# Root-mean-square norms over channels: a full-matrix mean on all partitions and a root by logarithm and exponential, in place of per-token columns and a broadcast

## The chip, the cores and the metric

The kernel runs on one core of a Trainium2 chip. The metric is device time in microseconds (us). Three runs of the kernel before took 2551.5, 2551.55 and 2554.44 us, so the median is 2551.55 us. One further run, of 2548.32 us, was profiled; its span, from the first to the last recorded instruction, is 2546.5 us. The engines are named as in the profile: PE (TensorE; PEld are its weight loads), DVE (VectorE), ACT (ScalarE), POOL (GpSimd), and SP, which only issues DMA transfers.

## The reference

One decoder layer over 2048 tokens of 1024 channels, all in float32. Four norms act on a token's 1024 channels: before the mixers, before the MLP, and at the end (three gains `g1`, `g2`, `g3`; the head norms over 64 channels are another routine that the change leaves alone).

```python
def rmsnorm(x, gain):
    y = x * lax.rsqrt(jnp.mean(x * x, axis=-1, keepdims=True) + EPS)
    return y * gain

h = rmsnorm(x, norm_mix_gain)             # 1
z = h @ w_in                              # 3072 columns, three mixers run on its parts
x = x + y @ w_out
x = x + conv_ffn(rmsnorm(x, norm_ffn_gain), w_up, conv_w, w_down)   # 2
x = x + sigmoid(x @ w_gate) * (p @ w_proj)
return rmsnorm(x, final_norm_gain)        # 3
```

## The kernel before

Channels lie on the 128 partitions (a token's 1024 channels are eight tiles, `KD = 8`) and tokens along the free axis. The 2048 tokens are two halves of `TH = 1024`, worked one after the other, and each half is two chunks of `CH = 512`. Every large product is three float32r matmuls (`mm3`, lines 261 to 264): both operands are split into a high and a low part, and the low times low product is left out. A split (`split`, line 253) is a rounding copy on ACT (line 255) and a subtraction on DVE or POOL (line 256). Weights are loaded on SP into the raw buffers `wr` (three) and `q` (three) and split two to three products ahead of their use (`w_get`, line 240).

A half has these stages:

- Input norm and projection. In half 0 the tokens are loaded at the start (`x_load`); `h_apply` (line 413) writes `hx = x * gain * rstd` on DVE (line 417) and splits it, some of the low parts on POOL. For half 1 the sums of squares are made from reloaded tokens while half 0 is in its MLP (`stats_steps`, line 980), and the norm is applied while half 0 is in its last stage. The projection is woven with the three mixers.
- Output projection (`out_evac`, line 760): x is reloaded by POOL's queue into `xr`, added to the product (line 765), squared for the second norm and stored by the same queue. While chunk 1 runs, the norm of chunk 0 is applied (`h2_first`); the norm of chunk 1 comes at the head of the MLP (`up_first`, line 881), where `h2_second` (line 786) forms normed tiles, their differences and their splits on DVE, ACT and POOL, and PE multiplies them as they come.
- MLP (`up`, `down_pair`, `down_last`), where PE has a long run of products.
- Gate, per-layer embedding and final norm (line 1036 on): two chunks of 512 tokens in half 0; 512, 256 and 256 in half 1. The last 256 tokens' norm ends the program.

There are 13 norms over channels, 11 of 512 tokens and 2 of 256: two at the start, two before the MLP in each half, two from `stats_steps`, two and three at the end of the halves. Each is an object of class `Norm`. `add` squares a tile on ACT and adds it to the accumulator on DVE or POOL. `rstd` multiplies each 128 tokens of the accumulator, as weights, by a column of ones (line 313), so that a token's sum lands on its own partition in a 128x4 tile; scale, root, reciprocal and a Newton step run there on DVE (lines 316 to 322) and ACT (line 317). `bcast` multiplies the root, repeated along the free axis as weights, by the identity (line 329), which puts it on all partitions in PSUM, where `pr` is read by line 417, 775 or 1028.

The order of instructions on each engine is set by a scheduler when the program is built; an engine takes its instructions strictly in that order. Small tiles (`hx`, `xr`, `xs`, squares) share the pool `sp` under the tag `t2`, four buffers.

Of the kernel before, what the change touches and what calls it, by code (L numbers as in the profile page):

```python
# [9 lines left out]
F32 = mybir.dt.float32  # L10
F32R = mybir.dt.float32r
I32 = mybir.dt.int32
AF = mybir.ActivationFunctionType
# [3 lines left out]
P = 128  # L17
# [3 lines left out]
CH = 512  # L21
NC = TH // CH
D = 1024
# [5 lines left out]
EPS = 1e-6  # L29
# [7 lines left out]
VOFF = {}  # L37
# [11 lines left out]
def trunk(ctx, tc, xT, pT, w_in, w_out, w_up, w_down, w_pp, w_pg, wr_bd, wi_bd, vecs, consts, masks, out):  # L49
    nc = tc.nc  # L50

    cp = ctx.enter_context(tc.tile_pool(name="cp", bufs=1))
    wp = ctx.enter_context(tc.tile_pool(name="wp", bufs=3))
    bp = ctx.enter_context(tc.tile_pool(name="bp", bufs=40))
    dp = ctx.enter_context(tc.tile_pool(name="dp", bufs=1, space=bass.MemoryType.DRAM))
    sp = ctx.enter_context(tc.tile_pool(name="sp", bufs=4))
    mm = ctx.enter_context(tc.tile_pool(name="mm", bufs=2, space=bass.MemoryType.PSUM))
    sm = ctx.enter_context(tc.tile_pool(name="sm", bufs=4, space=bass.MemoryType.PSUM))

    ACT = nc.scalar.activation  # L60
    TT = nc.vector.tensor_tensor
    TS = nc.vector.tensor_scalar
    STT = nc.vector.scalar_tensor_tensor
    MUL, ADD, SUB = ALU.mult, ALU.add, ALU.subtract
    MM = nc.tensor.matmul
# [3 lines left out]
    def nm(s):  # L69
        uid[0] += 1  # L70
        return f"{s}_{uid[0]}"

    def t4(name="t4", dt=F32):
        return bp.tile([P, TH], dt, tag="b", name=nm(name))
# [6 lines left out]
    def t2(name="t2"):  # L81
        return sp.tile([P, CH], F32, tag="t2", name=nm(name))
# [4 lines left out]
    def ps1(n=CH, name="ps1"):  # L87
        return sm.tile([P, n], F32, tag="sm", name=nm(name))
# [5 lines left out]
    pools = {}  # L94
# [39 lines left out]
        return kc(w_up[i * NJ + j])[:, QS[k]]  # L134

    def raw_q(src):
        raw = pools["ff"].tile([P, CH], F32, tag="q", name=nm("q"), bufs=3)
        dst = raw if len(src.shape) == 2 else raw.rearrange("p (a b) -> p a b", b=src.shape[2])
        nc.sync.dma_start(dst, src)
        return raw  # L140
# [50 lines left out]
    def last_job(hf, j):  # L191
        def load():
            raws[hf, j, 3] = raw_q(quarter(j, 1, 1))

        return (4, hf, j), load, lambda: one(raws[hf, j, 3])

    def down_jobs(hf, gi):
        js = GROUPS[gi]
        per = 4 // len(js)
        jobs = []  # L200
        for i in range(KD // per):
            def load(i=i):
                src = w_down[i * per : (i + 1) * per, :, js[0] : js[-1] + 1, :].rearrange("m p j c -> p m (j c)")
                raws[hf, gi, "d", i] = raw_q(src)
            jobs.append((("d", hf, gi, i), load, lambda i=i: one(raws[hf, gi, "d", i])))
        return jobs
# [22 lines left out]
    def w_upto(n):  # L229
        while wpos[1] < min(n, len(wlist)):  # L230
            key, _, make = wlist[wpos[1]]
            while wpos[0] <= wpos[1]:
                load = wlist[wpos[0]][1]
                wpos[0] += 1
                if load:
                    load()
            wpos[1] += 1
            wmade[key] = make()
# [14 lines left out]
    def split(hi, lo, src, eng=None):  # L253

        i = ACT(hi, src, AF.Copy)  # L255
        last_split[:] = i, (eng or nc.vector).tensor_tensor(lo, src, hi.bitcast(F32), op=SUB)  # L256
# [25 lines left out]
    ident = kt[:, KIDENT : KIDENT + P]  # L282
    onecol = kt[:, KONES : KONES + 1]
    blk = cp.tile([P, P], F32R, name="blk")
    vt = cp.tile([P, NV], F32, name="vt")

    def vec(name, i):
# [1 line left out]
        return vt[:, o : o + 1]  # L289

    epsc = cp.tile([P, 1], F32, name="epsc")


    class Norm:
# [4 lines left out]

        def add(self, src, eng=None, big=False):  # L300
            n = src.shape[-1]
            sq = (t4("sq") if big else t2("sq"))[:, :n]
            ACT(sq, src, AF.Square)
            if self.acc is not None:
                (eng or nc.vector).tensor_tensor(self.acc, self.acc, sq, op=ADD)
            else:
                self.acc = sq

        def rstd(self):
            n = self.acc.shape[-1] // P  # L310
            pm = ps1(n, "pm")
            for t in range(n):
                MM(pm[:, t : t + 1], self.acc[:, t * P : (t + 1) * P], onecol, start=True, stop=True)
            v = sp.tile([P, 16], F32, tag="tiny", name=nm("v"), bufs=4)
            m, r, s, u = (v[:, 4 * i : 4 * i + n] for i in range(4))
            TS(m, pm, 1.0 / D, EPS, op0=MUL, op1=ADD)
            ACT(s, m, AF.Sqrt)
            nc.vector.reciprocal(r, s)
            TT(u, r, r, op=MUL)
            TT(u, u, m, op=MUL)  # L320
            TS(u, u, -0.5, 1.5, op0=MUL, op1=ADD)
            TT(r, r, u, op=MUL)
            self.r = r

        def bcast(self):
            n = self.r.shape[-1]
            pr = ps1(n * P, name="pr")
            for t in range(n):
                MM(pr[:, t * P : (t + 1) * P], self.r[:, t : t + 1].to_broadcast([P, P]), ident, start=True, stop=True)
            return pr  # L330

    def head_norm(y, gain, scale=1.0):

# [95 lines left out]


    nc.vector.memset(epsc, EPS)
    warm = cp.tile([P, 1], F32, name="warm")
    ACT(warm, epsc, AF.Sqrt)
    h = [[None] * KD for _ in range(NC)]
    x0 = [[], []]

    def x_load(xs, hf, c, eng):

        t0 = hf * TH + c * CH
        for k in range(0, KD, 2):  # L440
            t = t4("xl")
            eng.dma_start(t.rearrange("p (k t) -> p k t", k=2), xT[k : k + 2, :, t0 : t0 + CH].rearrange("k p t -> p k t"))
            xs += [t[:, :CH], t[:, CH:]]
# [2 lines left out]
    nc.sync.dma_start(kt, consts[:, :KBLK])  # L446
    w_upto(1)
    nc.sync.dma_start(vt, vecs)
    w_upto(2)
    x_load(x0[1], 0, 1, nc.sync)  # L450
    norms = [Norm(), Norm()]
# [3 lines left out]
    pr = norms[0].bcast()  # L455
# [6 lines left out]
    for hf in range(NH):  # L462
# [5 lines left out]
        for i in range(NC):  # L468
            t = mx.tile([P, 8, P], F32, name=nm("acc"))
            nc.gpsimd.memset(t, 0.0)  # L470
            accs.append(t)
        for i in range(2):
            t = mx.tile([P, 8, 2, C], F32, name=nm("qz"))
# [256 lines left out]
        if first:  # L730
# [6 lines left out]
            t = t4("blk")[:, :P]  # L737
# [278 lines left out]
        for i in range(2):  # L1016
            raw = wp.tile([P, D], F32, tag="wr", name=nm("wr"))
# [18 lines left out]
        for ci, (t0, n) in enumerate(chunks):  # L1036
            c, o = t0 // CH, t0 % CH
            sl = slice(t0, t0 + n)
            raw, phi, plo = t4("pr"), t4("ph", F32R), t4("pl", F32R)
# [9 lines left out]
            for m in range(KD):  # L1049
# [6 lines left out]
                for k in range(KD):  # L1056
                    t = xs[c][k]
# [102 lines left out]
```

## Time and profile before

| | |
|---|---|
| median of three runs | 2551.55 us |
| profiled execution, its span | 2548.32 us, 2546.5 us |
| PE busy | 2454.9 us (96% of the span) |
| DVE busy | 1613.4 us (63%) |
| ACT busy | 1310.7 us (51%) |
| POOL busy | 237.2 us (9%) |
| mean granted TensorE clock | 0.987 of full speed |

Busy time is the time in which at least one instruction of the engine runs. Matmuls overlap in the trace: each of 512 columns lasts about 0.39 us, and the next begins 0.23 us after it. "Idle before" in square brackets is how long the engine had nothing to run ahead of a row, and the arrow names what ended it. A row with x4 stands for four instructions in a row.

### The profile page before, as it was taken

The numbers are of one execution on the slowest core, as the hardware profiler recorded it, in microseconds if no ns is written. First come the engines' busy times: TensorE is split into PE (matmuls) and PEld (weight loads), VectorE is DVE, ScalarE is ACT, GpSimd is POOL, SyncE is SP. The second block draws the span as 40 slices with busy tenths as digits, with TensorE's granted clock in tenths as the row PEclk, the third lists the DMA queues.
The fourth block names the chain that finished last, engine by engine and source line by source line (L and its number), as shares of the span: only waits on it lengthen the run. The fifth ranks groups of instructions, "written<-read, shape, count | busy, mean of one in ns | idle before, by whom it ended". The sixth has DMA issues, their size and how long they took to land. (4 is left out here: it accounts for less than half of the span.)

```text
span 2546.5 us, 30816 instructions
## 1 busy us (share of the span) xinstructions
PE 2454.9 (96%) x12004; PEld 2020.1 (79%) x12004; DVE 1613.4 (63%) x2384; ACT 1310.7 (51%) x1778; POOL 237.2 (9%) x278
## 2 busy tenths in 40 slices
PE   6999999899999999999999999997999999999998
PEld 4887788678888888887888887785888888888788
DVE  6666565685556566558666656567666666655776
ACT  5444884365555545555344457634555555555453
POOL 2000001201111111110110000012111111111100
PEclk9999999899999999999999999998999999999999
DMA  3101114346565555573421111251555555556642
GB/s 136 42 26 34 42 58 164 122 120 138 132 137 135 140 124 124 127 195 116 149 92 34 34 34 54 79 189 39 124 129 136 133 125 128 133 130 136 177 149 92
DMA packets 121170, 280.71 MB, mean 110 GB/s; under 512 B 11840, under 2 KB 42176, under 8 KB 121024
## 3 DMA queue, kind: packets, MB, share of 16 engines
q0 software_dynamic: 31360, 113.26, 21.3%
q1 hardware_dynamic: 88656, 164.30, 19.9%
q8 instruction: 94, 1.54, 0.2%
q10 hardware_dynamic: 1008, 1.18, 0.2%
q14 instruction: 52, 0.43, 0.1%
HBM read 178.03 MB, written 100.66 MB: 109 GB/s over the span
## 5 line engine op out<-in xcount | busy, mean ns | idle before, releaser
L262 PE MATMUL pz<-h,wh 128*128 128x512 f32 x768 | 306.3, 399 | 9.5 <-ACT h L255 9.5
L263 PE MATMUL pz<-h,wh 128*128 128x512 f32 x768 | 302.0, 394 | 1.2 <-DVE h L256 0.8
L264 PE MATMUL pz<-h,wl 128*128 128x512 f32 x768 | 300.6, 392 | 0.0
L262 PE MATMUL pdn<-ahi,wt 128*128 128x512 f32 x704 | 277.7, 394 | 12.6 <-DVE x L974 11.0
L264 PE MATMUL pa<-h,wt 128*128 128x512 f32 x704 | 276.5, 393 | 6.8 <-DVE wt L256 6.8
L262 PE MATMUL pa<-h,wt 128*128 128x512 f32 x704 | 276.3, 393 | 3.3 <-ACT wt L255 1.8
L263 PE MATMUL pdn<-alo,wt 128*128 128x512 f32 x704 | 275.8, 392 | 0.0
L264 PE MATMUL pdn<-ahi,wt 128*128 128x512 f32 x704 | 275.6, 392 | 0.0
L263 PE MATMUL pa<-h,wt 128*128 128x512 f32 x704 | 275.6, 391 | 0.0
L961 ACT ACTIVATE st<-pdn 128x1024 f32<-128x1024 f32 x160 | 164.0, 1026 | 210.5 <-PE pdn L264 189.9
L256 DVE TENSOR_TENSOR wt<-s,wt 128x512 fp32r<-128x512 f32 x168 | 114.1, 688 | 218.0 <-ACT wt L255 217.8
L962 POOL DMA_DIRECT2D xd<-st x160 | 136.9, 856 | 1087.4 <-ACT st L961 1084.3
L262 PEld LDWEIGHTS pz<-h,wh 128*128 128x128 f32 x768 | 144.8, 189 | 40.7 <-ACT h L255 10.7
L263 PEld LDWEIGHTS pz<-h,wh 128*128 128x128 f32 x768 | 144.8, 189 | 33.0 <-DVE h L256 4.1
L262 PEld LDWEIGHTS pdn<-ahi,wt 128*128 128x128 f32 x704 | 133.2, 189 | 45.6 <-DVE x L974 13.9
L264 PEld LDWEIGHTS pz<-h,wl 128*128 128x128 f32 x768 | 144.8, 189 | 30.1 <-issue 0.3
L256 DVE TENSOR_TENSOR wl<-wr,wh 128x1024 fp32r<-128x1024 f32 x120 | 146.2, 1227 | 35.1 <-ACT wh L255 34.7
L264 PEld LDWEIGHTS pa<-h,wt 128*128 128x128 f32 x704 | 133.3, 189 | 35.3 <-DVE wt L256 7.7
L262 PEld LDWEIGHTS pa<-h,wt 128*128 128x128 f32 x704 | 133.1, 189 | 33.0 <-ACT wt L255 2.7
L264 PEld LDWEIGHTS pdn<-ahi,wt 128*128 128x128 f32 x704 | 133.2, 189 | 28.0
L263 PEld LDWEIGHTS pa<-h,wt 128*128 128x128 f32 x704 | 133.1, 189 | 27.6
L263 PEld LDWEIGHTS pdn<-alo,wt 128*128 128x128 f32 x704 | 133.3, 189 | 27.1
(271 smaller groups left out, 5170.0 us busy)
## 6 DMA issues: line engine op xcount, KB each, us to landing
xd<-st POOLq DMA_DIRECT2D x160, 512.0 KB, 6.1
wr<-in_w_up SPq DMA_DIRECT2D x176, 256.0 KB, 4.1
wr<-in_w_in SPq DMA_DIRECT2D x48, 512.0 KB, 3.7
q<-in_w_down SPq DMA_DIRECT2D x88, 256.0 KB, 3.4
wr<-in_w_pg SPq DMA_DIRECT2D x40, 512.0 KB, 4.5
wr<-in_w_out SPq DMA_DIRECT2D x32, 512.0 KB, 3.8
q<-in_w_up SPq DMA_DIRECT2D x42, 256.0 KB, 3.0
xr<-in_xT POOLq DMA_DIRECT2D x32, 256.0 KB, 3.9
```

Source lines behind the costliest of these rows:

```text
L256: last_split[:] = i, (eng or nc.vector).tensor_tensor(lo, src, hi.bitcast(F32), op=SUB)
L262: MM(ps, wk[0], rk[0], start=start, stop=False, **kw)
L263: MM(ps, wk[0], rk[1], start=False, stop=False, **kw)
L264: MM(ps, wk[1], rk[0], start=False, stop=stop, **kw)
L961: ACT(st, ps, AF.Copy)
L962: nc.gpsimd.dma_start(xd[m], st, accum_op=ADD)
```

## The change

`Norm.add` gives the accumulator buffers of its own (tag `acc`, four of 512 columns); the first square goes there. `rstd` splits the accumulator into two float32r parts and multiplies both by a 128x128 matrix of 1/1024 (`ones`), so that the mean stands on all partitions for all tokens at once, in one PSUM tile. From it ACT forms the logarithm, the exponential of minus a half of it times a constant, and its square; two DVE instructions over the whole tile are a Newton step for the root. The sign comes out negative, so the three gains are negated once at the start. `bcast` returns the accumulator, in SBUF, and has no instructions. The pool `sp` goes from four buffers to three and `q` from three to two.

```diff
-    sp = ctx.enter_context(tc.tile_pool(name="sp", bufs=4))
+    sp = ctx.enter_context(tc.tile_pool(name="sp", bufs=3))
...
-        raw = pools["ff"].tile([P, CH], F32, tag="q", name=nm("q"), bufs=3)
+        raw = pools["ff"].tile([P, CH], F32, tag="q", name=nm("q"), bufs=2)
...
         def add(self, src, eng=None, big=False):
             n = src.shape[-1]
-            sq = (t4("sq") if big else t2("sq"))[:, :n]
+            if self.acc is None:
+                sq = sp.tile([P, CH], F32, tag="acc", name=nm("acc"), bufs=4)[:, :n]
+            else:
+                sq = (t4("sq") if big else t2("sq"))[:, :n]
             ACT(sq, src, AF.Square)
...
         def rstd(self):
-            n = self.acc.shape[-1] // P
+            n = self.acc.shape[-1]
+            t = t4("sqs", F32R)
+            split(t[:, :n], t[:, CH : CH + n], self.acc)
             pm = ps1(n, "pm")
-            for t in range(n):
-                MM(pm[:, t : t + 1], self.acc[:, t * P : (t + 1) * P], onecol, start=True, stop=True)
-            v = sp.tile([P, 16], F32, tag="tiny", name=nm("v"), bufs=4)
-            m, r, s, u = (v[:, 4 * i : 4 * i + n] for i in range(4))
-            TS(m, pm, 1.0 / D, EPS, op0=MUL, op1=ADD)
-            ACT(s, m, AF.Sqrt)
-            nc.vector.reciprocal(r, s)
-            TT(u, r, r, op=MUL)
-            TT(u, u, m, op=MUL)
-            TS(u, u, -0.5, 1.5, op0=MUL, op1=ADD)
-            TT(r, r, u, op=MUL)
-            self.r = r
+            MM(pm, ones, t[:, :n], start=True, stop=False)
+            MM(pm, ones, t[:, CH : CH + n], start=False, stop=True)
+            ACT(self.acc, pm, AF.Ln, bias=epsc)
+            ACT(self.acc, self.acc, AF.Exp, scale=-0.5, bias=lnc)
+            u = t4("nr")[:, :n]
+            ACT(u, self.acc, AF.Square)
+            STT(u, pm, EPS, u, op0=ADD, op1=MUL)
+            STT(self.acc, u, 1.5 * 2.0 ** (1 / 3), self.acc, op0=SUB, op1=MUL)
 
         def bcast(self):
-            n = self.r.shape[-1]
-            pr = ps1(n * P, name="pr")
-            for t in range(n):
-                MM(pr[:, t * P : (t + 1) * P], self.r[:, t : t + 1].to_broadcast([P, P]), ident, start=True, stop=True)
-            return pr
+            return self.acc
...
+    nc.vector.memset(lnc, -np.log(2.0) / 3)
     warm = cp.tile([P, 1], F32, name="warm")
-    ACT(warm, epsc, AF.Sqrt)
+    ACT(warm, epsc, AF.Square)
+    t = t2("ones")[:, :P]
+    nc.vector.memset(t, 1.0 / D)
+    ACT(ones, t, AF.Copy)
...
     nc.sync.dma_start(vt, vecs)
+    TS(vt[:, VOFF["g1"] : VOFF["gm"]], vt[:, VOFF["g1"] : VOFF["gm"]], -1.0, None, op0=MUL)
```

Lines of the changed kernel behind the class `Norm` have numbers seven to nine higher. The order of the instructions, at three places. First ACT at the start of the program, before the change: `wh` are split weights, `xl` the loaded tokens (`xl_111` to `xl_117` are chunk 1), `v` the 128x4 tile, `h` the split normed tokens of chunk 0.

```order
L255 ACTIVATE wh_100<-wr_98 128x1024
L317 ACTIVATE v_147<-v_147 128x4
L255 ACTIVATE wh_107<-wr_105 128x1024
L303 ACTIVATE sq_160<-xl_111 128x512
L303 ACTIVATE sq_180<-xl_117 128x512
L255 ACTIVATE h_185<-hx_183 128x512
```

The same place after it (`xl_118` to `xl_124` are chunk 1, `acc_126` is chunk 0's accumulator, `acc_161` that of chunk 1; as above, the squares between the first and the last are left out):

```order
L255 ACTIVATE wh_114<-wr_112 128x1024
L308 ACTIVATE acc_161<-xl_118 128x512
L255 ACTIVATE sqs_149<-acc_126 128x512
L322 ACT_TABLE_LOAD
L322 ACTIVATE acc_126<-pm_152,epsc 128x512
L325 ACT_TABLE_LOAD
L325 ACTIVATE acc_126<-acc_126,lnc 128x512
L327 ACTIVATE nr_157<-acc_126 128x512
L308 ACTIVATE sq_163<-xl_118 128x512
L308 ACTIVATE sq_181<-xl_124 128x512
L255 ACTIVATE h_186<-hx_184 128x512
```

The norm of chunk 0 now has a square of chunk 1 ahead of it on ACT, and seven squares of chunk 1 stand between it and the first split of `hx`. Second, DVE at the same place, before and after: `wl` are the low parts of the weights.

```order
L305 TENSOR_TENSOR sq_119<-sq_119,sq_139 128x512
L316 TENSOR_SCALAR v_147<-pm_142 128x4
L256 TENSOR_TENSOR wl_101<-wr_98,wh_100 128x1024
L318 RECIPROCAL v_147<-v_147 128x4
L322 TENSOR_TENSOR v_147<-v_147 128x4
L256 TENSOR_TENSOR wl_108<-wr_105,wh_107 128x1024
L417 SCALAR_TENSOR_TENSOR hx_183<-xl_89,vt,pr_155 128x512
```

```order
L310 TENSOR_TENSOR acc_126<-acc_126,sq_146 128x512
L455 TENSOR_SCALAR vt<-vt 128x24
L256 TENSOR_TENSOR wl_107<-wr_104,wh_106 128x1024
L256 TENSOR_TENSOR wl_115<-wr_112,wh_114 128x1024
L256 TENSOR_TENSOR sqs_149<-acc_126,sqs_149 128x512
L328 SCALAR_TENSOR_TENSOR nr_157<-pm_152,nr_157 128x512
L329 SCALAR_TENSOR_TENSOR acc_126<-nr_157,acc_126 128x512
L419 SCALAR_TENSOR_TENSOR hx_184<-xl_95,vt,acc_126 128x512
```

The first weights' low part no longer stands behind an instruction of the norm. Third, ACT at the head of the MLP of half 1, where the second norm before the MLP is made (`zg`, `zu` are evacuated products, `pa` their PSUM tiles, `x_12430` and `x_12389` the last tile of x); before, then after:

```order
L303 ACTIVATE sq_12781<-x_12430 128x512
L317 ACTIVATE v_12817<-v_12817 128x4
L890 ACTIVATE zu_12798<-pa_12795 128x512
L895 ACTIVATE zg_12797<-pa_12794 128x512
L255 ACTIVATE h_12849<-h_1925_12540 128x512
```

```order
L308 ACTIVATE sq_12734<-x_12389 128x512
L902 ACTIVATE zg_12750<-pa_12747 128x512
L255 ACTIVATE sqs_12765<-acc_12428 128x512
L322 ACT_TABLE_LOAD
L322 ACTIVATE acc_12428<-pm_12768,epsc 128x512
L325 ACT_TABLE_LOAD
L325 ACTIVATE acc_12428<-acc_12428,lnc 128x512
L327 ACTIVATE nr_12773<-acc_12428 128x512
L897 ACTIVATE zu_12751<-pa_12748 128x512
```

An evacuation (line 902) now stands ahead of the norm on ACT, the norm has four passes over 512 columns and two table loads, and the other evacuation stands behind it.

## Rows read from the trace of the kernel before

**Rows 1.** Busy time by stretch: PE, PEld, DVE, ACT, POOL, clock, DMA share, GB/s

```profile
560.00:1000.00 440.00, 439.02 (x1938) 362.52 (x1937) 254.76 (x352) 229.63 (x312) 53.90 (x63) 1.00 0.59 134
1720.00:1760.00 40.00, 29.04 (x118) 21.53 (x119) 30.04 (x42) 14.31 (x25) 15.06 (x11) 0.88 0.09 33
```

**Rows 2.** Timeline of PE around a broadcast: start, us, engine, line, operation

```profile
1687.54 1.05 PE L329 MATMUL pr<-kt,v 128*128 128x128 f32 x8
1688.35 0.48 PE L262 MATMUL po<-ys,wh 128*128 128x512 f32 x1
1688.66 0.40 PE L263 MATMUL po<-ys,wh 128*128 128x512 f32 x1
1688.89 0.39 PE L264 MATMUL po<-ys,wl 128*128 128x512 f32 x1
```

**Rows 3.** Timeline of the start: SP, ACT, DVE and PE

```profile
12.21 1.87 PE L313 MATMUL pm<-kt,sq 128*128 128x1 f32 x8 [12.21 <-DVE sq L305]
14.19 1.23 DVE L256 TENSOR_TENSOR wl<-wr,wh 128x1024 fp32r<-128x1024 f32 x1
15.82 2.06 SPq L442 DMA_DIRECT2D xl<-in_xT  x4
20.93 1.15 ACT L303 ACTIVATE sq<-xl 128x512 f32<-128x512 f32 x2 [5.47 <-DMA xl<-in_xT]
26.28 2.17 ACT L255 ACTIVATE h<-hx 128x512 fp32r<-128x512 f32 x4
26.95 0.80 PE L262 MATMUL pz<-h,wh 128*128 128x512 f32 x1 [8.52 <-ACT h L255]
39.16 2.36 DVE L256 TENSOR_TENSOR wl<-wr,wh 128x1024 fp32r<-128x1024 f32 x2 [0.26 <-ACT wh L255]
45.26 0.74 PE L262 MATMUL pz<-h,wh 128*128 128x512 f32 x2 [0.57 <-ACT h L255]
```

**Rows 4.** Groups of instructions by line and form: busy us, mean ns of one

```profile
L256 DVE TENSOR_TENSOR sqp<-sqh,sqp 128x512 fp32r<-128x512 f32 x32 | 21.0, 686 | 7.6 <-ACT sqp L255 7.6
L343 ACT ACTIVATE sqh<-pmh,epsc 128x512 f32<-128x512 f32 x32 | 20.6, 685 | 11.7 <-PE pmh L352 11.6
L345 ACT ACT_TABLE_LOAD x18 | 23.1, 1283 | 0.3
L345 ACT ACTIVATE sqh<-sqh 128x512 f32<-128x512 f32 x32 | 18.7, 624 | 0.2
L346 DVE SCALAR_TENSOR_TENSOR dv<-dv,ms,sqh 128x512 f32<-128x512 f32 x12 | 8.7, 749 | 30.8 <-ACT sqh L345 30.8
```

**Rows 5.** Timeline of DVE and PE, head of the MLP of half 1

```profile
1728.04 0.69 DVE L305 TENSOR_TENSOR sq<-sq,sq 128x512 f32<-128x512 f32 x1 [0.75 <-ACT sq L303]
1728.79 1.05 PE L313 MATMUL pm<-kt,sq 128*128 128x1 f32 x8
1733.64 0.75 DVE L775 SCALAR_TENSOR_TENSOR h<-x,vt,pr 128x512 f32<-128x512 f32 x1 [2.36 <-PE pr L329]
1756.97 0.79 PE L262 MATMUL pbc<-h,wt 128*128 128x512 f32 x1 [6.69 <-DVE zg L905]
```

**Rows 6.** Timeline of POOL and DVE, the same stage

```profile
1741.52 6.82 POOL L803 TENSOR_TENSOR h<-h,h 128x512 f32<-128x512 f32 x4 [13.28 <-DVE h L775]
1742.02 0.74 DVE L775 SCALAR_TENSOR_TENSOR h<-x,vt,pr 128x512 f32<-128x512 f32 x1
1742.67 1.12 DVE L256 TENSOR_TENSOR h<-h,h 128x512 fp32r<-128x512 f32 x1
1747.13 1.76 DVE L802 TENSOR_TENSOR h<-h,h 128x512 f32<-128x512 f32 x1
```

**Rows 7.** Timeline of DVE at the end of the program

```profile
2535.24 0.43 DVE L305 TENSOR_TENSOR sq<-sq,sq 128x256 f32<-128x256 f32 x1 [0.48 <-ACT sq L303]
2539.53 3.22 DVE L1028 SCALAR_TENSOR_TENSOR o<-x,vt,pr 128x256 f32<-128x256 f32 x8 [1.32 <-PE pr L329]
```

**Rows 8.** Loads into `q`, issue to landing

```profile
DMA to landing us min/median/max: 2.6/3.2/10.8
```

More of the change, by code (lines that the diff above doesn't have):

```diff
@@ L284, in trunk @@
     blk = cp.tile([P, P], F32R, name="blk")
+    ones = cp.tile([P, P], F32R, name="ones")
     vt = cp.tile([P, NV], F32, name="vt")
@@ L291, in trunk @@
     epsc = cp.tile([P, 1], F32, name="epsc")
+    lnc = cp.tile([P, 1], F32, name="lnc")
     class Norm:
```

## The prediction

> **What bounds the kernel now.** I read the busy shares first, then busy time by stretch, then the waits of PE, then the timeline at each place where PE waits. PE is busy for 2454.9 of 2546.5 us, so about 92 us are left, and the stretches say where. In the MLP PE has no room: 439.02 of 440 us [rows 1]. At the head of the MLP of half 1 it is busy for 29.04 of 40 us, while DVE has 30.04 [rows 1], and PE's longest wait there, 6.69 us, is for DVE [rows 5]. The start is alike: the first product begins at 26.95 us, after a wait for ACT [rows 3]. So a norm over channels is paid in two ways. Where PE is full, it costs the PE time of its own matmuls. Where PE waits for the normed tiles (the start, the head of the MLP in both halves, and the end of the program), it costs the length of its chain through DVE, ACT and PE. The change makes the first smaller and the second longer.
>
> **PE's own time.** A broadcast takes PE from 1687.54 to 1688.35, and the matmul behind it is followed after 0.31 us instead of 0.23: 0.81 + 0.08 = 0.89 us [rows 2]. The sum over channels has eight records too, over the same 1.05 us [rows 2, 5], and I take the same 0.89. The two new matmuls of 512 columns cost 2 x 0.23 = 0.46 [rows 2]. A norm of 512 tokens so gives PE 1.32 us, one of 256 tokens 0.66. Where PE is full stand two norms from `stats_steps`, two at the end of half 0, and in half 1 one of 512 and one of 256: 5 x 1.32 + 0.66 = **7.3 us less**. The other seven stand where PE waits for their result, or for the reloads of x in the output projection, which are one POOL transfer after another. If all thirteen gave their PE time it would be 11 x 1.32 + 2 x 0.66 = 15.8; nothing is the other bound.
>
> **The start.** Two things happen. The first weights' low part waited on DVE behind line 316, which waits for the sum (12.21 to 14.1); now it stands directly behind the adds, so `wl` begins 1.9 us earlier than 14.19, its raw buffer comes free earlier, and so do the loads of chunk 1 queued on SP behind it (15.82): they land from 19.0 instead of 20.93 [rows 3]. But ACT now has a square of chunk 1 ahead of chunk 0's norm, so that norm cannot begin before 19.0, and seven more squares stand behind it ahead of the first split of `hx`. From 19.0: a square 0.58 (half of 1.15, rows 3), copy 0.62, low part 0.69, two matmuls 0.8 (as the first one at 26.95), logarithm 0.69, table load 1.28, exponential 0.62, square 0.58, seven squares 4.0 [rows 3, 4]. That is 28.9, with four handovers of 0.06 (1728.73 to 1728.79, rows 5) 29.1, where before it was 26.28 [rows 3]: 2.9 later. The second norm was spread under the splits: the weights' low parts ended at 41.52, and PE had chunk 1 at 45.26, 3.7 later [rows 3]. In the new order the whole norm stands behind those splits: low part 0.69, matmul 0.4, logarithm 0.69, load 1.28, exponential 0.62, square 0.58, two Newton steps at 0.75, `hx` 0.75, its copy 0.62, and eight handovers: 7.6, so 3.9 more. To these 6.8 I add 1.2 for `hx` meeting POOL (next part): **8 us more**. Bounds: 3.9, if the first delay is hidden, and 11, if each `hx` of both chunks loses a turn to POOL. PE has then two products' worth of chunk 0 to do and runs dry, so nothing hides it.
>
> **The head of the MLP, twice.** Before, from the last add's end (1728.73) to the first `hx` (1733.64) pass 4.9 us [rows 5]. Now: copy 0.62, low part 0.69, the low part's matmul 0.4, logarithm 0.69, table load 1.28, exponential 0.62, square 0.58, two Newton steps 1.5, eight handovers 0.5, and half of the evacuation (0.3) that now stands ahead on ACT: 7.2, **2.3 us more**. The first table load is under the wait for the sum. Behind this chain DVE works nearly without a gap until PE gets its tiles at 1756.97, so I let it through in full.
> In that stage `hx` changes its operand from PSUM to SBUF. While POOL runs its four differences (6.82 us, 1.7 each), an `hx` that reads `pr` in PSUM takes 0.74, no more than alone; a subtraction that reads two SBUF tiles takes 1.12 to 1.76, where it takes 0.69 alone [rows 4, 6]. So DVE and POOL take turns when DVE has two SBUF inputs, and the `hx` ran in POOL's turn for nothing. Three of the eight `hx` of the stage lie there. With the accumulator in SBUF they need turns of their own: 3 x 0.66 = **2.0 us more**. Bounds: nothing, if the scalar form of instruction is exempt, and 3 x (1.76 - 0.74) = 3.1. No row shows that form with two SBUF inputs beside POOL; I take the middle since the 1.12 row is the nearest. Together 4.3 us a half, 8.6 in all.
>
> Two rules of the Trainium skill bear on these sums, and both differ from the trace. Line 346 multiplies two float32 tiles in SBUF in the same form as the new `hx` and takes 749 ns for 512 columns, as much as the one from PSUM (0.74) [rows 4, 6]. The skill (Vector Engine (DVE) Microarchitecture Reference, Points that are easy to get wrong) says that a scalar_tensor_tensor with two SBUF sources that are not bf16 runs at half throughput; by it every `hx` would take some 0.7 us more, and the sum would be that of the last rival; the row contradicts it. For the tables, the row shows a load of 1.28 us between the logarithm and the exponential of the head norms, 18 times [rows 4]. The skill (ScalarE: Activation LUTs, What ACT_TABLE_LOAD costs) has the logarithm and then the exponential in one set with one load; by it each exposed chain would be 1.28 shorter, five times, and the sum about 6 us smaller. The order of the changed kernel has both loads, so the trace's price stands.
>
> **The end.** From the last add's end (2535.67) to the first output 3.86 us pass [rows 7]. With 256 columns at 0.42 to 0.45 a pass (the add's 0.43, rows 7): copy, low part, matmuls 0.5, logarithm, load 1.28, exponential, square, two Newton steps: 4.8, with nine handovers 5.4: **1.5 us more**.
>
> **Costed at nothing.** The pool `sp` loses a buffer, but the accumulator that held one of the four has moved out, so as many are left for `hx`, `xr` and `xs`. In the MLP and in the last stages a norm gives ACT four wide passes and a second load; ACT is at half load there, and PE has a second PSUM tile to fill meanwhile; without that cover each such norm would cost about 3 us. `q` with two buffers: a load is issued when the split two before it is done, not three; it lands in 3.2 us at the median, 10.8 at worst [rows 8], and splits run about three products, some 8 us, ahead of PE. If that lead is used up, see the third rival.
>
> **Sum.** -7.3 + 8.0 + 8.6 + 1.5 = +10.8 us. On the profiled execution's 2548.3 that is 2559.1. The median of the runs shown lies 3.2 us above that execution; on it, the forecast is 2562 us. About 0.2%, 5 us, is what a measurement of this kernel tells from no change.
>
> **Rivals.**
> 1. The other side, faster: the long chains hide and PE's saving counts at every norm. For it: PE is busy 96% of the time. Against it: PE waits exactly where the chains end [rows 3, 5]. It needs the DVE work behind the chain to have slack of over 4 us in each half. Then -15.8 + 1.5 for the end, about -14: 2537 us. Chance 0.11. It decides as soon as the two heads together add less than the matmuls save.
> 2. `hx` from SBUF doesn't wait for POOL: 4.0 and 1.2 us fall away, +5.6: 2557 us. For it: no row shows the form beside POOL. Against: the turns of the two-input subtractions. Chance 0.20.
> 3. The loads into `q` come late in the MLP: ACT, strictly in order, stands before a split whose load was issued too late, and the later splits with it, about 0.8 us for each of 24 groups of down products, +19 more: 2581 us. For it: landings of up to 10.8. Against: the lead. Chance 0.06.
> 4. `hx` at half rate everywhere: 32 of them on the chains by 0.7, +22: 2584 us. Line 346's row speaks against it. Chance 0.03.
> The forecast itself has 0.60.
>
> **Range and chances.** The forecast's own bounds are those of the start (4 to 11), the heads (2.3 to 5.4 each) and PE's time (0 to -10), which rarely meet at one end: 2549 to 2575. It takes in rival 2 and leaves out rivals 1, 3 and 4, 0.20. Faster by over 0.2% is rival 1 and a little of the forecast's lower edge, 0.13. Within 0.2% (2546 to 2557) is part of rival 2 and the lower part of the forecast, 0.17. Slower 0.70.
>
> **What would show it.** In the new profile the first product should begin near 29 us instead of 26.95 and chunk 1's near 53 instead of 45.26; at the head of the MLP the first `hx` 7 us behind the last add, and `hx` beside POOL at 1.1 us or more; the first output 5.4 us behind the last add; the MLP of both halves as full as before. The forecast is wrong if `hx` stays at 0.74 beside POOL, if PE's waits at the heads don't grow, or if PE shows new waits for splits of `q` in the MLP.

## The result, and the profile after

The changed kernel takes 2591.36 us (median of four runs, 2590.22 to 2592.33), the kernel before 2551.53 us beside it: a ratio of 1.0155, interval 1.014 to 1.0171. The forecast was 2562 us, range 2549 to 2575. The direction was right and the size was not: 39.8 us instead of 10.8. The profiled execution has a span of 2589.6 us, 43.1 us over before, where the profiled execution was 3.2 us faster than the median of its runs.

PE's busy time hardly changed (2456.0 after 2454.9 us), so the time is in its waits. Where they lie is seen by taking the same matmul in both traces and subtracting its start times. The lag grows like this, by stage (worked out from the records of PE, us; the stage "start" ends with the first `pd` product of the mixers, and a profile of one kernel differs from another of the same work by up to some 3 us in the MLP of half 0):

```
stage, up to ...                                   lag at its end   added
start, up to the first pd product of half 0              13.5       13.5
mixers of half 0, to the output projection               13.8        0.3
output projection and head of the MLP                    23.2        9.3
MLP of half 0, to the first gate product                 27.8        4.6
last stage of half 0 and first products of half 1        28.6        0.8
mixers of half 1                                         29.5        0.9
output projection and head of the MLP                    38.6        9.2
MLP of half 1                                            39.5        0.8
last stage of half 1, to its last gate product           41.4        1.9
the end                                                  43.0        1.6
```

The start comes first; these are rows of ACT, POOL, DVE and PE picked from the timeline of the changed kernel (start us, duration, engine, line, out<-in, count, and in brackets what ended the idle time). They answer to [rows 3].

```profile
18.63 0.63 ACT L308 ACTIVATE acc<-xl 128x512 f32<-128x512 f32 x1 [5.35 <-DMA xl<-in_xT]
...
22.09 1.28 ACT L325 ACT_TABLE_LOAD   x1
24.68 3.73 ACT L308 ACTIVATE sq<-xl 128x512 f32<-128x512 f32 x7
25.38 11.32 POOL L310 TENSOR_TENSOR acc<-acc,sq 128x512 f32<-128x512 f32 x7 [21.02 <-ACT sq L308]
25.53 1.66 DVE L329 SCALAR_TENSOR_TENSOR acc<-nr,acc 128x512 f32<-128x512 f32 x1
27.22 4.99 DVE L419 SCALAR_TENSOR_TENSOR hx<-xl,vt,acc 128x512 f32<-128x512 f32 x3
28.90 0.63 ACT L255 ACTIVATE h<-hx 128x512 fp32r<-128x512 f32 x1 [0.49 <-DVE hx L419]
29.58 0.80 PE L262 MATMUL pz<-h,wh 128*128 128x512 f32 x1 [8.23 <-ACT h L255]
33.94 0.80 PE L263 MATMUL pz<-h,wh 128*128 128x512 f32 x1 [3.56 <-DVE h L256]
...
55.38 1.22 PE L262 MATMUL pz<-h,wh 128*128 128x512 f32 x2 [5.01 <-ACT h L255]
57.76 0.75 DVE L419 SCALAR_TENSOR_TENSOR hx<-xl,vt,acc 128x512 f32<-128x512 f32 x1 [1.16 <-POOL h L256]
```

The first product is 2.6 us late, where 2.9 were forecast. But its last step is not the forecast one: the seven squares end at 28.41, and the split behind them then waits for the first `hx` until 28.90. The last instruction of the Newton step (line 329) and three `hx` take 1.66 us each beside POOL, so PE's second matmul waits until 33.94 (28.07 before), and chunk 1 is 10.1 us late.

At the head of the MLP of half 1, the same view, DVE, ACT and PE; it answers to [rows 5, 6]:

```profile
1761.97 0.69 DVE L310 TENSOR_TENSOR acc<-acc,sq 128x512 f32<-128x512 f32 x1 [0.75 <-ACT sq L308]
...
1765.94 1.28 ACT L325 ACT_TABLE_LOAD   x1
1768.52 0.58 ACT L897 ACTIVATE zu<-pa 128x512 f32<-128x512 f32 x1
1768.64 0.69 DVE L328 SCALAR_TENSOR_TENSOR nr<-pm,nr 128x512 f32<-128x512 f32 x1 [4.22 <-ACT nr L327]
1769.15 0.50 PE L262 MATMUL pa<-h,wt 128*128 128x512 f32 x1 [1.90 <-ACT zu L897]
1770.10 1.42 DVE L782 SCALAR_TENSOR_TENSOR h<-x,vt,acc 128x512 f32<-128x512 f32 x2
1773.76 0.60 ACT L906 ACTIVATE zu<-pa 128x512 f32<-128x512 f32 x1 [4.66 <-PE pa L264]
1774.25 1.14 ACT L255 ACTIVATE h<-h 128x512 fp32r<-128x512 f32 x2
...
1780.10 1.77 DVE L782 SCALAR_TENSOR_TENSOR h<-x,vt,acc 128x512 f32<-128x512 f32 x1
1781.79 0.68 DVE L256 TENSOR_TENSOR h<-h,h 128x512 fp32r<-128x512 f32 x1
```

From the last add's end (1762.66) to the first `h` (1770.10) pass 7.44 us, 2.5 more than before. Then ACT has an evacuation (line 906) ahead of the copies of `h`. It waits for a product that PE could only begin at 1769.15, since the evacuation before it (line 897) stood behind the norm on ACT: from the first `h` to 1780.10 pass 10.0 us, 1.6 more than before. The three `h` beside POOL take 1.77 instead of 0.74, their low parts 0.68 instead of 1.12: 1.8 more by 1787.

In half 0 the chain is longer: from the last add's end to the first `h` pass 9.1 us (495.97 to 505.09) against 4.9 before, 4.2 more. Two squares of the first statistics norm stand on ACT between the copy and the logarithm there (496.90 and 497.79), and one of its additions on DVE ahead of the first `h`.

One place that the forecast held to be covered is the first statistics norm in the MLP of half 0. ACT, DVE and PE of the changed kernel:

```profile
818.38 1.28 ACT L322 ACT_TABLE_LOAD   x1
...
820.38 1.28 ACT L325 ACT_TABLE_LOAD   x1
...
822.41 1.28 ACT L874 ACT_TABLE_LOAD   x1
...
824.67 0.61 ACT L327 ACTIVATE nr<-acc 128x512 f32<-128x512 f32 x1
825.32 0.69 DVE L328 SCALAR_TENSOR_TENSOR nr<-pm,nr 128x512 f32<-128x512 f32 x1 [3.77 <-ACT nr L327]
825.71 1.92 ACT L968 ACTIVATE st<-pdn 128x1024 f32<-128x1024 f32 x2
826.77 0.50 PE L262 MATMUL pdn<-ahi,wt 128*128 128x512 f32 x1 [2.05 <-ACT st L968]
...
828.74 0.63 PE L263 MATMUL pdn<-alo,wt 128*128 128x512 f32 x1
```

The evacuation `st` stands on ACT behind the norm and three table loads (the SiLU's own table comes in between), and PE waits 2.05 us for it. The second statistics norm does the same, with a wait of 2.06 us at 1070.62; before, no wait of PE for `st` was longer than 1.0. Then PE pays again: its matmuls follow each other after 0.43 us instead of 0.23. The window behind it, from the table by stretch (window, its length, busy time and count of PE, PEld, DVE, ACT, POOL, then the granted clock), has half clock, 1.2 of 2.4 GHz:

```profile
828.20:831.60 3.40, 3.40 (x9) 2.62 (x9) 0.67 (x1) 0.48 (x1) 0.70 (x1) 0.50 1.03 183
```

With 3.4 us at half clock, 1.7 us of work are lost, nearly as much as the wait. Over the program the mean granted clock went from 0.987 to 0.982. As a stretch is granted either full or half, that is 2 x 0.018 x 2589.6 = 93 us at half clock against 2 x 0.013 x 2546.5 = 66, part of it in PE's waits.

### The profile page after: what moved, and what is told of

It is laid out like the page before. It is cut to its first block, busy times and chain, and to the rows that moved or that the text cites. A ratio compares the mean times of both kernels' runs of the same rounds, so it can differ in the third digit from the quotient of the medians.

```text
span 2589.6 us, 30494 instructions
## 1 busy us (share of the span) xinstructions
PE 2456.0 (95%) x11838; PEld 2011.4 (78%) x11838; DVE 1636.2 (63%) x2348; ACT 1362.3 (53%) x1834; POOL 240.9 (9%) x278
## 3 DMA queue, kind: packets, MB, share of 16 engines
q0 software_dynamic: 31360, 113.26, 20.8%
## 4 chain that ended last, share of the span: by engine, by line
PE 71%; issue 9%; DVE 8%; ACT 8%; DMA 2%; POOL 1%; SPq 0%; DVEq 0%; POOLq 0%; ACTq 0%
PE pa L264 5%; PE pa L262 5%; PE pa L263 5%; PE pdn L262 5%; PE pdn L263 5%; PE pdn L264 5%; PE pz L262 5%; PE pz L263 5%; PE pz L264 5%; PE pb L264 2%; PE pb L262 2%; PE pb L263 2%; PE pl L642 2%; PE pgt L264 2%; PE pgt L263 2%
```

## The experiments

Each kernel is timed beside the kernel before on the same chip; ratios are to that one, and "under" means under the changed kernel's 2591.36 us. The runs beside the kernel before were made on several chips, where it took 2549.77 to 2551.53 us. By the ratios the same differences come out up to 3 us smaller (e3 7.4, e4 19.4, e5 13.5, e6 24.5, e11 6.6, e12 29.6) or, for e9, 1 larger (20.4).

**e1: the kernel before, with ACT as busy as after.**

```diff
             ACT(s, m, AF.Sqrt)
+            d = t4("d")[:, : self.acc.shape[-1]]
+            ACT(d, self.acc, AF.Copy)
+            ACT(d, self.acc, AF.Ln, bias=epsc)
+            ACT(d, d, AF.Exp, scale=-0.5)
+            ACT(d, d, AF.Square)
```

> The kernel before, with four more passes on ScalarE behind the root of every norm (copy, logarithm, exponential, square of the accumulator into a scratch tile that nothing reads); the norm's own result doesn't wait for them. They hold ScalarE as long as the new norm does, about 5.2 us with two table loads. Theory A (a wide norm costs because evacuations and splits stand behind it on ScalarE): the two norms of the statistics in the MLP cost some 3 us each, the evacuations at the heads about 2 us a half, the output projection 1 to 4 us a half: 2562 to 2570 us. Theory B (only the length of the chain to the normed tiles counts, ScalarE has room): at most 2 us more, 2551 to 2554 us.

Measured: 2558.64 us, ratio 1.0036 (1.0024 to 1.0049), 8.3 us over before: between the two theories, and A's places were wrong. In its trace the start adds 7.9 us, the output projection and heads -0.4 and 1.3, the MLP of half 0 -0.6, the last stage of half 1 2.0. So at the heads and in the MLP ACT's occupancy by itself costs next to nothing, though the run has 124 table loads against 96 before, 36 us of ACT's time more. These passes differ from the new norm's in two ways, which the run doesn't part: nothing waits for them, and they wait for no sum. At the first statistics norm the copy and the logarithm with its load come ahead of the pass at 804.17 that forms `gu`, and `st` follows that pass after 5.0 us. In the changed kernel the logarithm and the exponential, their loads and the SiLU with its own stand between the two, and it takes 8.5 us (817.21 to 825.71). PE's waits in the MLP of half 0 are no longer than before:

```profile
PE pdn L262 <- DVE x L979: 5.2, 2, 4.3
PE pdn L262 <- ACT st L966: 1.2, 3, 0.9
```

**e2: the kernel before, with the changed buffer counts.**

```diff
-    sp = ctx.enter_context(tc.tile_pool(name="sp", bufs=4))
+    sp = ctx.enter_context(tc.tile_pool(name="sp", bufs=3))
-        raw = pools["ff"].tile([P, CH], F32, tag="q", name=nm("q"), bufs=3)
+        raw = pools["ff"].tile([P, CH], F32, tag="q", name=nm("q"), bufs=2)
```

> The kernel before with only the buffer counts of the changed one (three t2 tiles with the accumulators still among them, two q tiles). Theory A (the buffers cost nothing, the loss is in the chains and on ScalarE): within 3 us of before for q; the accumulators still sit in the t2 ring here, so a loss in the output projection of up to 5 us a half says nothing against it. Theory C (q loads come late in the MLP, the prediction's third rival): 15 us or more, with waits of PE for splits of q in the MLP.

Measured: 2558.45 us, 1.0037 (1.0025 to 1.005). This misses the 3 us. One reason is seen that the changed kernel doesn't share: with the accumulators still in the ring, ACT waits for tokens of the statistics. Its trace, of an execution 6.4 us over the run's median, adds 7.2 us in the MLP of half 0, where these waits lie, but also 4.5 at the start and 6.1 in the output projection and head of half 1, which no run explains. For `q` ACT waits 21 times, 1.2 us on average; no wait of this kind is seen before, and the changed kernel has it too. These are ACT's waits in e2 (for what: us in total, times, longest):

```profile
ACT wt L255 <- DMA q<-in_w_down: 25.2, 21, 2.3
ACT sq L303 <- DMA xs<-in_xT: 17.4, 5, 6.1
```

In the changed kernel:

```profile
ACT wt L255 <- DMA q<-in_w_down: 22.8, 20, 3.2
ACT sq L308 <- DMA xs<-in_xT: 5.6, 6, 2.4
```

PE doesn't feel the waits for `q`: in the MLP of half 1 the lag grows by 0.8 us after the change and 0.2 in e2. Theory C is out. The change with the old buffer counts was not run.

**e3: `hx` reads the root from PSUM.**

```diff
-            STT(self.acc, u, 1.5 * 2.0 ** (1 / 3), self.acc, op0=SUB, op1=MUL)
+            self.acc, acc = (self.acc if hold else pm), self.acc
+            STT(self.acc, u, 1.5 * 2.0 ** (1 / 3), acc, op0=SUB, op1=MUL)
...
-                n.rstd()
+                n.rstd(True)
```

> The changed kernel, with the last Newton step of all norms but the two statistics in the MLP writing into the PSUM tile of the mean, so that hx reads one SBUF and one PSUM operand as before. Theory A (DVE and POOL take turns where DVE has two SBUF inputs): hx beside POOL falls from 1.7 to 0.74 us; at the heads 1.8 us a half come back, at the start 4 to 7 us: 2579 to 2584 us. Rival (the turn lost by hx is only handed on to the low part behind it): 2588 to 2592 us.

Measured: 2582.88 us, 1.0126 (1.011 to 1.0141), 8.5 us under the changed kernel, within A's range, though not at A's places in half 1. DVE's timeline in e3, at the start and at the head of half 1:

```profile
25.63 1.67 DVE L330 SCALAR_TENSOR_TENSOR pm<-nr,acc 128x512 f32<-128x512 f32 x1
27.33 2.06 DVE L420 SCALAR_TENSOR_TENSOR hx<-xl,vt,pm 128x512 f32<-128x512 f32 x3
...
1774.22 0.73 DVE L783 SCALAR_TENSOR_TENSOR h<-x,vt,pm 128x512 f32<-128x512 f32 x1
1774.88 1.10 DVE L256 TENSOR_TENSOR h<-h,h 128x512 fp32r<-128x512 f32 x1
```

Both forms stand beside POOL: with two SBUF inputs 1.67 us, with one in PSUM 0.69 and 0.73. At the start 4.6 us come back, in the output projection and head of half 0 3.1. In half 1 the head itself, from the last add to PE's product behind its wait for `zg`, is 1.8 us shorter (32.4 instead of 34.2), but the stage with its output projection adds 9.0 us as against 9.2.

**e4: the old form at the heads.** In `out_evac`'s stage `norms = [Norm(True), Norm(True)]`, where `True` selects the old `rstd` and `bcast` (root made negative, for the negated gains).

> The changed kernel with the old form of the norm (narrow sum, narrow root, broadcast on TensorE) at the four norms of the output projection and of the head of the MLP, the new form elsewhere. Theory A (what the difference of the two traces puts on these places, 9.3 us a half, is caused there): 2591 - 18.6, about 2573 us (2569 to 2577). Rival (the delay there is handed on from the start or is given back later): 2582 us or more.

Measured: 2570.58 us, 1.0079 (1.0066 to 1.0091), 20.8 us under the changed kernel. The stage adds -2.8 and 0.1 us instead of 9.3 and 9.2. So what these stages lose is caused by their own four norms, and isn't handed on from the start.

**e5: no Newton step.** The square, the two DVE steps and the negated gains are taken out.

> The changed kernel without the Newton step: the reciprocal root is what logarithm and exponential give (the square on ScalarE and the two steps on VectorE are left out, the gains keep their sign). Theory A (VectorE, in order, stands before the first Newton step until ScalarE is through, and what is queued behind it waits too): each of the five chains that PE waits for is 2.2 us shorter, and in the output projection and the statistics VectorE no longer stands there: 11 to 18 us less, 2573 to 2580 us. Rival (what costs is ScalarE's table loads and passes, with the evacuations behind them; the Newton step lies beside them): 4 us less at most, 2587 us or more.

Measured: 2574.7 us, 1.0102 (1.0085 to 1.0119), 16.7 us under, within A's range. The run takes a pass of ACT out together with the two of DVE, and doesn't tell which of them counts.

**e6: no table loads.**

```diff
-            ACT(self.acc, pm, AF.Ln, bias=epsc)
-            ACT(self.acc, self.acc, AF.Exp, scale=-0.5, bias=lnc)
+            ACT(self.acc, pm, AF.Copy, scale=1e-2)
+            ACT(self.acc, self.acc, AF.Copy, scale=0.5)
```

> The changed kernel with plain scaled copies in place of the logarithm and of the exponential, so that the same passes run without their two table loads; the root isn't computed, and the outputs aren't the reference's. Theory A (a chain costs by its length): one load of 1.28 us is exposed at each of five chains and at the two norms in the output projection, the other one lies under the wait for the sum, and some 1.3 us of evacuation come back at each statistics norm: 9 to 12 us less, 2579 to 2582 us. Rival (the loads are hidden everywhere but in the five chains' sum): 3 us less at most, 2588 us or more.

Measured: 2564.22 us, 1.0059 (1.0048 to 1.0071): 27.1 us under the changed kernel. Both theories had it far too small. The run takes out more than the 26 loads of the norms: it has 80 table loads where the changed kernel has 112, since six at other functions (the gates of the last stage, the SiLU, the mixers) fall away too. That is 41 us of loads. It has 16 loads fewer than the kernel before and is still 14.5 us slower, so the loads are not all of the loss. The gain is in every stage where a norm stands: start 4.1 us, heads 7.5 and 6.6, MLP of half 0 8.7, last stage and end of half 1 4.3.

**e9: one of the two loads.** As e6, with the logarithm kept.

> The changed kernel with the logarithm kept and a scaled copy in place of the exponential: one table load a norm instead of two, all passes kept; the root isn't computed, and the outputs aren't the reference's. With both loads gone 27 us came back. Theory A (the exponential's load is the one that is exposed, since the logarithm's lies under the wait for the sum): 15 to 22 us less than the changed kernel, 2569 to 2576 us. Rival (both loads are in the way alike, behind other work of ScalarE): 13 us less, about 2578 us. If only the chains' own length counted, 7 x 1.28 = 9 us less, 2582 us.

Measured: 2572.0 us, 1.0075 (1.0062 to 1.0089), 19.4 us under: A. The expectation counts one load a norm; the trace has fewer. These are the loads of the norm by line: the square root's before, then the logarithm's and the exponential's in the changed kernel, then the logarithm's in e9 (count, busy us, ns of one):

```profile
L317 ACT ACT_TABLE_LOAD x9 | 11.5, 1283 | 0.2
```

```profile
L322 ACT ACT_TABLE_LOAD x13 | 16.7, 1283 | 0.3
L325 ACT ACT_TABLE_LOAD x13 | 16.7, 1283 | 0.2
```

```profile
L322 ACT ACT_TABLE_LOAD x10 | 12.8, 1283 | 0.3
```

Without the exponential three of the logarithm's loads go too, and one comes in elsewhere: 97 loads in all, 15 fewer than in the changed kernel, 19.2 us of loads for 19.4 us of time. So these loads are paid about in full. The 17 further loads that e6 drops, 21.8 us, give back only 7.8 (4.1 by the ratios). The old norm was not free of loads either: the change adds 16 to the program's 96, not 26. DVE's wait before the first Newton step follows: first the changed kernel, then e9, then e6.

```profile
DVE nr L328 <- ACT nr L327: 48.9, 13, 5.5
```

```profile
DVE nr L328 <- ACT nr L327: 29.2, 13, 4.3
```

```profile
DVE nr L326 <- ACT nr L325: 19.2, 10, 2.8
```

**e7 and e8: another order at the start of the kernel before.** e8 is the same with `None` (VectorE) for `nc.gpsimd`.

```diff
-    for k in range(KD):
-        norms[1].add(x0[1][k], nc.gpsimd, True)
-    run(h_apply(h[0], x0[0], "g1", pr))
+    for k, _ in enumerate(h_apply(h[0], x0[0], "g1", pr)):
+        norms[1].add(x0[1][k], nc.gpsimd, True)
```

> The kernel before, with chunk 1's squares and their additions written between chunk 0's products of the gain rather than ahead of all of them, so that ScalarE makes a split of chunk 0 before each square of chunk 1. Theory A (at the start ScalarE stands before squares whose data lands at 20.9 us, with the splits of chunk 0 behind them from 19.2 on): first product at 20 to 21 us instead of 26.95, chunk 1's norm at about the same time as before: 2 to 5 us less, 2546 to 2549 us. Rival (chunk 1's norm comes later by what chunk 0 gains, and PE waits there): 2550 to 2554 us.

> As e7_before_order, with chunk 1's additions on VectorE instead of POOL. Theory A (POOL's seven additions of 1.5 us make the low parts of chunk 0 take 1.5 instead of 0.69 us, and this costs more than VectorE's own seven of 0.69): 1 to 3 us below e7. Rival (VectorE is what paces chunk 0): 1 to 4 us above e7.

Measured: e7 2546.53 us, 0.9989 (0.998 to 0.9998); e8 2543.02 us, 0.9975 (0.9964 to 0.9985). e8 beats both kernels. In e8's trace ACT splits at once and PE begins at 19.84 instead of 26.95 [rows 3]:

```profile
19.15 0.63 ACT L255 ACTIVATE h<-hx 128x512 fp32r<-128x512 f32 x1 [3.79 <-DVE hx L417]
20.92 0.63 ACT L303 ACTIVATE sq<-xl 128x512 f32<-128x512 f32 x1 [1.14 <-DMA xl<-in_xT]
...
19.84 0.79 PE L262 MATMUL pz<-h,wh 128*128 128x512 f32 x1 [1.50 <-ACT h L255]
40.47 1.22 PE L262 MATMUL pz<-h,wh 128*128 128x512 f32 x2 [1.50 <-ACT h L255]
```

The profiled spans of the two are equal (2543.4 and 2543.8), so whether e8 is better than e7 stays open.

**e10: the last norm of half 0 ahead of half 1's second splits.**

```diff
         if not last:
+            before[1].rstd()
             run(h_apply(hn[1], xn[1], "g1", nstats[1].bcast(), (1, 3, 5, 7)))
-        before[1].rstd()
+        else:
+            before[1].rstd()
```

> The changed kernel with the last norm of half 0 written ahead of the splits of half 1's second chunk instead of behind them, so that ScalarE makes the accumulator's copy before those splits. Theory A (TensorE, in order, stands 3.4 us before that norm's sum, whose high part is queued on ScalarE behind the splits): that wait goes, 3 to 5 us less, 2586 to 2588 us. Rival (the splits of half 1 then come later by the norm's chain, and TensorE waits for them instead): 2590 to 2594 us.

Measured: 2589.44 us, 1.0149 (1.0135 to 1.0163): neither, 2 us under the changed kernel with overlapping intervals. In the changed kernel PE, in order, stands before this norm's sum:

```profile
1325.98 0.50 PE L320 MATMUL pm<-sqs,ones 128*128 128x512 f32 x1 [3.43 <-ACT sqs L255]
```

In e10 that wait is gone and PE waits for half 1's tiles instead, by its waits in this stage:

```profile
PE pz L263 <- POOL h L256: 2.0, 2, 1.3
PE pz L262 <- ACT h L255: 0.6, 1, 0.6
PE pz L263 <- DVE h L256: 0.5, 1, 0.5
```

**e11: the old form at the two statistics norms.** `n = Norm(True)` in `stats_steps`.

> The changed kernel with the old form at the two norms of the statistics in the MLP of half 0 alone. Theory A (each of them makes TensorE wait some 2 us for the evacuation of pdn, and lose as much again at half clock behind it): 5 to 6 us less, 2585 to 2587 us, and the clock granted around both places is full. Rival (these norms lie beside other work, and what the trace shows there is made up for later): 2590 to 2592 us.

Measured: 2583.8 us, 1.0129 (1.0115 to 1.0142), 7.6 us under, a little over A. Its stretches around both places, by the same table as above, are full and at full clock:

```profile
810.00:830.00 20.00, 20.00 (x93) 16.35 (x92) 12.28 (x21) 10.52 (x13) 2.41 (x3) 1.00 0.33 70
1050.00:1070.00 20.00, 20.00 (x92) 16.35 (x92) 12.85 (x21) 10.52 (x13) 1.80 (x3) 1.00 0.34 79
```

**e12: the remedies together.** The edits of e5, e10 and the start of e8 on the changed kernel; `ACT(pm, acc, AF.Exp, ...)` writes into PSUM.

> The changed kernel with what the runs so far point to put together: no Newton step, the exponential writing into the PSUM tile of the mean (statistics norms aside), the last norm of half 0 ahead of half 1's second splits, and at the start chunk 1's squares between chunk 0's splits with the additions on VectorE. The two table loads stay. If the gains add up (16.7 for the Newton step, 4 for PSUM at the heads, 3 for the order, 2 for the start): 2563 to 2567 us, still slower than before by what the loads cost. If the parts overlap: 2568 to 2573 us.

Measured: 2560.57 us, 1.0039 (1.0026 to 1.0051), 30.8 us under, 5.1 more than the 25.7 of the expected sum, so below both expected ranges. Its parts include all of e3's edit, which alone gave 8.5 and not the 4 that were counted; they overlap, and no run parts them. It is still slower than before, and slower by 17.5 us than e8, which has the start's order and the old norm.

## Why the prediction was wrong, point by point

By the table of lags the traces lie 32 us above the sum. Of these 5.5 are at the start, 9.9 in the two stages with the heads, and 16.6 in the rest (MLPs, mixers, last stages), where I had put -7.3 and 9.3 were measured.

- **PE's own time, -7.3 us: right in size where it can be seen.** With two broadcasts fewer in the last stage of half 0, the lag falls from the first gate product to the first products of half 1 by 4.3 us after the change, and by 2.5 in e11, which still has those two broadcasts: 0.9 us each, as taken from [rows 2].
- **The start, +8.0: too small, 13.5.** The first chain's length was right (first product at 29.58, forecast some 29), with some luck: ACT reached the split by the forecast steps at 28.41, and an `hx` that POOL had slowed, which is not among those steps, set the end. The 1.2 us for meeting POOL were the mis-sized term: an `hx` beside POOL takes 1.66, not 1.1, the Newton step is caught too, and chunk 1's `hx` wait behind POOL's low parts (3.5 us in all). e3 gives back 4.6 of it by the operand alone.
- **The heads, 2.3 + 2.0 a half: both terms right in half 1 (2.5 and 1.8), and the sum wrong.** 9.3 and 9.2 were measured. The 1.8 is net of something that I hadn't seen: an `h` beside POOL loses 1.03, not 0.66, and the low part behind it gains 0.44. In half 0 the chain is 4.2 longer, not 2.3, with work of the statistics norm inside it. In half 1 the evacuations behind the norm add 1.6, and 4.4 grow before it, in the output projection, at the norm that I had put under the reloads of x; 1.1 of it all come back behind the head.
- **The end, +1.5: right.** From the last add's end (2577.08) to the first output 5.46 us pass, forecast 5.4 [rows 7].

```profile
2576.66 0.42 DVE L310 TENSOR_TENSOR acc<-acc,sq 128x256 f32<-128x256 f32 x1 [0.48 <-ACT sq L308]
2582.54 2.86 DVE L1035 SCALAR_TENSOR_TENSOR o<-x,vt,acc 128x256 f32<-128x256 f32 x7
```

- **"Costed at nothing": the step that failed.** I priced a norm's chain only where PE waits for its result, and put the other norms under ACT's half load, PE's second PSUM tile and the reloads. That cover isn't there, and the sign that I gave for it, MLPs as full as before, fails in half 0. "Without that cover each such norm would cost about 3 us", and the statistics norms cost 3.8 each (e11). ACT's load alone, by which I judged that cover, doesn't decide: in e1 as many passes, waiting for no sum and waited for by nobody, cost nothing in the MLP. In the changed kernel DVE, in order, stands before the first Newton step for 48.9 us in all, 13 times, and the evacuations stand on ACT behind the chain.
- **The table loads: right price, wrong count.** 1.28 us each holds. I let one load count at five chains, 6.4 us. The program has 112 loads after the change and 96 before; taking the norm's away gives back 27.1 us (e6, 32 loads fewer), about two thirds of the whole loss, and taking the exponential's away 19.4 (e9, 15 fewer). The others, most of them the logarithm's, which I put wholly under the sum, give back 4 to 8. The Trainium skill (ScalarE: Activation LUTs, Table sets: the hidden batching unit; the prediction names the section before it) has a set that holds both functions, so that a logarithm and then an exponential need one load. The trace has two at each norm (26 for the 13), so no run here shows that; e9 stands nearest to it, with a copy in place of the exponential.
- **The clock: left out.** The new waits of 2.05 and 2.06 us at the statistics norms and of 3.43 us before the last norm of half 0 each have a stretch of 3.4 us at half clock at their end or just behind; at the first 2.05 us of wait brought 1.7 us of slow work. Not every new wait has one: none follows those of 2.17 us at 488.06 and of 1.76 at 1171.02.
- **The rivals.** Rival 2 (`hx` doesn't wait for POOL) is refuted by e3's rows. The Trainium skill (SBUF — State Buffer, SBUF: two separate sides) has the port pair that DVE and POOL share held for a whole instruction when a DVE instruction has two SBUF inputs and POOL's reads SBUF; 1.67 against 0.69 us agrees. Rival 3 (late `q`) has its waits on ACT but none on PE. Rival 4 (half rate) is out: alone the form takes 0.69 to 0.75 us. Rival 1 needed slack behind the chains, and the stages with the heads show none.
- **The range.** Its stated bounds add up to 0.1 and 23.3 us, 2552 to 2575, so the lower end of 2549 isn't theirs. The upper end held nothing for the norms costed at nothing.

What stays open is how the 4 us in the output projection come about. Three turns of the loop of reloads took 5.7, 6.6 and 6.3 us in half 1 and take 7.2, 8.1 and 7.0, with x waiting for `xr` up to 1.6 us. Two of the three loads into `xr` behind these turns take longer, 5.5 and 5.2 us from issue to landing against 3.6 and 4.5, and the first x itself stands on DVE behind the Newton step. It shrinks with the chain (e6: the whole stage adds 1.8 and 2.6 us), but no run took the loop alone. A Newton step placed behind the next add of x was not tried.

## What to carry to other kernels

Price a chain of small instructions on every engine that must stand in order behind one of its steps, not only where its result is waited for: here 13 norms cost time in nearly every stage, though PE needed the result in five places. A function whose table isn't loaded costs its load each time it alternates with another; count the loads in the order of instructions, those of the old form and of other functions too, and take each at full price where something stands in order behind it. An operand moved from PSUM to SBUF can lose more than the instruction that made it saves, if POOL works beside it.

## What the runs showed of the hardware that was not expected

- A two-input DVE instruction from SBUF took 1.66 us beside POOL, 0.97 more than alone, close to POOL's own 1.62 an instruction (11.32 / 7); the same form with one PSUM operand paid nothing (0.69).
- Fifteen table loads fewer, 19.2 us of an engine that is busy for 53% of the span, made the program 19.4 us shorter (e9). Twenty-eight more, 36 us with 52 passes besides, cost 8.3 us where they waited for no sum and nothing waited for them (e1).
- Writing the squares of one chunk between the splits of another, with no instruction less, made the tuned kernel 0.1% faster (e7, 0.998 to 0.9998), and with the additions on DVE 0.25% (e8, 0.9964 to 0.9985).
